# Two feed-forward column groups' first products among the last token transposes of a two-layer encoder, and half-sums formed per token tile

## The chip, the cores and the metric

One NeuronCore of a Trainium2 chip runs the whole two-layer network in one launch. The metric is the device time of one execution in microseconds (us), taken as the median over runs of the same program. Engines are written as in the profile: PE is TensorE, PEld its weight loads, DVE VectorE, ACT ScalarE, POOL GpSimd, SP the engine that issues the DMAs.

## The reference, cut to what matters

Each of two layers does, for 1024 tokens of width 1024 in float32:

```python
h = rms_norm(x, g_mix_pre)
u = h @ w_in                                   # attention, convolution, retention inputs
mix = jnp.concatenate([y_att, y_conv, y_ret], axis=-1) @ w_out
x = x + rms_norm(mix, g_mix_post)
h = rms_norm(x, g_mlp_pre)
f = jnp.square(jax.nn.relu(h @ w_up)) @ w_down # w_up: 1024 x 4096, w_down: 4096 x 1024
return x + rms_norm(f, g_mlp_post)
```

The change touches the stretch from `mix @ w_out` to the beginning of `h @ w_up`, in both layers.

## The kernel before

Tokens are worked on in eight tiles of 128 (t = 0 to 7); tiles 0 to 3 are the first token half, 4 to 7 the second. A float32 product is made of three matmuls on rounded parts: every operand is split into a high part (ACT casts it) and a low part (DVE subtracts the high part), and `mm3` (lines 147 to 151) issues high by high (L149), high weights by low moving (L150), low weights by high moving (L151).

**Output projection, right half.** The loop over the eight tiles under `Quarters(hblocks)` issues, for each tile, 24 matmuls of 128x512. Then the tile goes through a chain: ACT copies the result and sums its squares, DVE and POOL scale by the gain (`residual`, L235), POOL and DVE make the root-mean-square factor, DVE adds the residual (L240, with the old x loaded on SP's queue), ACT sums squares again, POOL makes the second factor, DVE scales to h (L208), PE transposes h in eight 128x128 blocks (L216), and ACT and DVE store the result (`Quarters.put`). The transposes carry a priority that moves them behind by `LAG`; a list scheduler, which simulates the program, places all instructions on each engine.

**Feed-forward up, `feed_up`.** The 1024x4096 weights are taken in eight column groups q of 512, and each group's product with h transposed is a fast 2x2 block product with seven half-size products instead of eight. The operands are quartered by row half and token half (`quarters.raw[j, n]`: row half j, token half n). Products 1 and 2 use the plain quarters of the first token half, so they need tiles 0 to 3 only. Products 3 to 7 use sums: on the moving side t1 to t4 and the plain quarter b22 (`moving_sums`, each 128x2048 sum and each split made as one DVE or ACT instruction, once per layer), on the weights' side s1, s2 and two more (`stationary_sums` and `last_sum`, four POOL instructions of 128x1024 per group, L290 and L287). One product is 24 matmuls of 128x512 into a pair of PSUM banks; a group is seven of them. The splits of weights and sums are all made by `parts_of` (ACT L294, DVE L295). `open_psum(4)` gives up all eight banks at once and takes them anew as four pairs a, b, c, d.

**Feed-forward down, `feed_down`.** It multiplies the seven results of each pair of groups, kept in DRAM, with the quarters of `w_down`; its accumulators are taken from the blocks of the feed-forward pool and first written by an ACT copy (L519).

Blocks are 128x2048 tiles of SBUF: 13 kept ones (`kb`), and 12 (`fb`) that live only in the feed-forward part. The mixer's result `mix` and the keys `kT` have their own pools per layer.

## Time and profile before

| | us |
|---|---|
| median of 3 runs | 2391.28 (2389.43 to 2391.61) |
| the profiled execution, its own time | 2391.76 |
| its span, first to last instruction | 2390.0 |
| PE busy | 2295.0 (96%) |
| DVE busy | 1630.6 (68%) |
| ACT busy | 1036.9 (43%) |
| POOL busy | 611.0 (26%) |
| mean granted clock of PE | 0.981 |

The page cuts the span into 40 slices of 59.75 us; a digit is the busy share in tenths. An idle time in the timeline stands in square brackets, with the instruction that ended it behind an arrow. A matmul's duration in the timeline is modelled and overlaps the next one's; the pace is read from the starts. The granted clock of 1.00 is 2.4 GHz, 0.50 is 1.2 GHz.

### The profile page before, as it was taken

What the parts mean: (1) busy time and instruction counts of PE and PEld (TensorE: products, weight loads), DVE (VectorE), ACT (ScalarE), POOL (GpSimd) and SP (SyncE); (2) the same over time, 40 slices, a digit from 0 to 9 for tenths busy, and PEclk for the clock granted to TensorE, in tenths of its full rate; (3) what the DMA queues carried; (4) which work ended last, traced back from release to release, by engine and by line L of the source; (5) the groups of instructions that cost most, each with busy time, mean ns of one, the idle gap of its engine ahead of it and who ended that gap; (6) DMA issues with size and microseconds to landing.
All of it is one profiled execution on the core that took longest, in us unless ns stands there. A gap on an engine that the chain in (4) does not pass through costs nothing.

```text
span 2390.0 us, 29843 instructions
## 1 busy us (share of the span) xinstructions
PE 2295.0 (96%) x11132; PEld 1885.7 (79%) x11132; DVE 1630.6 (68%) x2726; ACT 1036.9 (43%) x1745; POOL 611.0 (26%) x511
## 2 busy tenths in 40 slices
PE   8999999996999999999899999999969999999997
PEld 7887778775888887888788887787758888878886
DVE  6976776668554577577789676755785444766787
ACT  4234443564444454343332344535744444543332
POOL 1002222224565541000220122222245564400002
PEclk9999999997999999999999999999979999999998
DMA  5120110142344454434431210101424443554435
GB/s 180 49 67 6 32 36 1 54 150 88 136 173 146 154 209 178 176 123 159 154 116 49 67 32 5 36 1 54 168 75 171 145 159 138 211 185 159 146 137 167
DMA packets 108337, 268.29 MB, mean 112 GB/s; under 512 B 9608, under 2 KB 17824, under 8 KB 108192
## 3 DMA queue, kind: packets, MB, share of 16 engines
q1 hardware_dynamic: 108192, 266.39, 32.5%
q8 instruction: 87, 1.43, 0.3%
q14 instruction: 58, 0.48, 0.1%
HBM read 190.84 MB, written 75.52 MB: 111 GB/s over the span
## 4 chain that ended last, share of the span: by engine, by line
PE 41%; DVE 3%; issue 3%; POOL 2%; ACT 1%; DMA 1%; DVEq 0%; SPq 0%; ACTq 0%; POOLq 0%
PE pb L149 12%; PE pb L151 12%; PE pb L150 12%; PE pb L817 2%; DVE fb L240 1%; PE pb L804 1%; POOL kb L287 1%; PE pb L777 1%; PE pb L774 0%; PE pb L919 0%; PE pb L909 0%; POOL fb L287 0%; DVE fb L208 0%; POOL fb L290 0%; DVE kb L287 0%
## 5 line engine op out<-in xcount | busy, mean ns | idle before, releaser
L151 PE MATMUL pb<-kb,kb 128*128 128x512 f32 (+1 forms) x1600 | 623.7, 391 | 11.6 <-DVE kb L295 11.3
L149 PE MATMUL pb<-kb,kb 128*128 128x512 f32 (+1 forms) x1472 | 599.4, 409 | 5.5 <-ACT fb L519 2.4
L150 PE MATMUL pb<-kb,kb 128*128 128x512 f32 (+1 forms) x1536 | 598.8, 390 | 0.4 <-DVE kb L131 0.4
L290 DVE TENSOR_TENSOR fb<-pb,fb 128x1024 f32<-128x1024 f32 x174 | 212.7, 1223 | 276.4 <-PE pb L151 241.7
L151 PEld LDWEIGHTS pb<-kb,kb 128*128 128x128 f32 x1600 | 304.0, 190 | 74.2 <-DVE kb L295 13.6
L150 PEld LDWEIGHTS pb<-kb,kb 128*128 128x128 f32 x1536 | 293.6, 191 | 44.9 <-DVE kb L131 1.2
L149 PEld LDWEIGHTS pb<-kb,kb 128*128 128x128 f32 x1472 | 281.3, 191 | 58.1 <-issue 4.1
L149 PE MATMUL pb<-fb,kb 128*128 128x512 f32 x736 | 287.6, 391 | 13.9 <-ACT kb L294 13.9
L151 PE MATMUL pb<-fb,kb 128*128 128x512 f32 x704 | 273.7, 389 | 0.0
L150 PE MATMUL pb<-fb,kb 128*128 128x512 f32 x672 | 262.3, 390 | 1.3 <-DVE fb L295 1.3
L294 ACT CAST kb<-kb 128x1024 fp32r<-128x1024 f32 (+1 forms) x100 | 141.0, 1414 | 254.8 <-PE pb L150 150.1
L294 ACT CAST kb<-fb 128x1024 fp32r<-128x1024 f32 (+1 forms) x80 | 106.6, 1332 | 217.1 <-PE pb L150 134.8
L295 DVE TENSOR_TENSOR kb<-fb,kb 128x1024 fp32r<-128x1024 f32 (+1 forms) x72 | 139.2, 1933 | 77.0 <-ACT kb L294 76.9
L295 DVE TENSOR_TENSOR kb<-kb,kb 128x1024 fp32r<-128x1024 f32 (+1 forms) x78 | 152.0, 1951 | 37.5 <-ACT kb L294 37.4
L149 PEld LDWEIGHTS pb<-fb,kb 128*128 128x128 f32 x736 | 138.6, 188 | 43.1 <-ACT kb L294 14.7
L838 DVE SCALAR_TENSOR_TENSOR mix<-ypad,cw,mix 128x512 f32<-128x512 f32 x240 | 167.1, 751 | 1.0
L235 POOL TENSOR_TENSOR fb<-fb,fb 128x512 f32<-128x512 f32 x14 | 20.4, 1464 | 527.5 <-DMA fb<-in_norm_mlp_post_dram 254.1
L151 PEld LDWEIGHTS pb<-fb,kb 128*128 128x128 f32 x704 | 132.1, 188 | 27.5
L150 PEld LDWEIGHTS pb<-fb,kb 128*128 128x128 f32 x672 | 126.3, 188 | 28.5 <-DVE fb L295 2.3
L294 ACT CAST fb<-kb 128x2048 fp32r<-128x2048 f32 x42 | 80.3, 1913 | 112.5 <-DMA kb<-fd 59.2
L149 PE MATMUL pb<-kb,fb 128*128 128x512 f32 x320 | 124.5, 389 | 0.0
L131 DVE TENSOR_TENSOR kb<-kb,kb 128x512 fp32r<-128x512 f32 (+2 forms) x160 | 103.2, 658 | 28.2 <-ACT kb L130 26.1
(190 smaller groups left out, 4057.6 us busy)
## 6 DMA issues: line engine op xcount, KB each, us to landing
fd<-fb SPq DMA_DIRECT2D x80, 512.0 KB, 2.6
kb<-fd SPq DMA_DIRECT2D x36, 1024.0 KB, 4.9
fb<-in_w_up_dram SPq DMA_DIRECT2D x22, 1024.0 KB, 5.6
kb<-in_w_down_dram SPq DMA_DIRECT2D x44, 512.0 KB, 5.1
...
fb<-fd SPq DMA_DIRECT2D x20, 1024.0 KB, 5.0
fd<-kb SPq DMA_DIRECT2D x32, 512.0 KB, 3.5
kb<-in_w_up_dram SPq DMA_DIRECT2D x10, 1024.0 KB, 5.6
```

Source lines behind the costliest of these rows:

```text
L131: nc.vector.tensor_tensor(out=lo[:, :ncols], in0=raw[:, :ncols], in1=hi[:, :ncols].bitcast(F32), op=ALU.subtract)
L149: nc.tensor.matmul(ps, lhsT=a_hi, rhs=b_hi, start=first, stop=False, skip_group_check=more)
L150: nc.tensor.matmul(ps, lhsT=a_hi, rhs=b_lo, start=False, stop=False, skip_group_check=more)
L151: nc.tensor.matmul(ps, lhsT=a_lo, rhs=b_hi, start=False, stop=last, skip_group_check=more)
L240: nc.vector.scalar_tensor_tensor(out=xt[:, cs], in0=zs[c], scalar=r, in1=xt[:, cs], op0=ALU.mult, op1=ALU.add)
L287: eng.tensor_tensor(out=out, in0=a, in1=b, op=ALU.subtract)
L290: eng.tensor_tensor(out=out, in0=a, in1=b, op=ALU.add)
L294: nc.scalar.copy(hi, raw)
L295: nc.vector.tensor_tensor(out=lo, in0=raw, in1=hi.bitcast(F32), op=ALU.subtract)
L777: nc.tensor.matmul(ps[hh], lhsT=self.qs[hs, hh, :], rhs=klo[hs, ks], start=False, stop=True)
L817: nc.tensor.matmul(ops, lhsT=sb[:, j * P:(j + 1) * P], rhs=V[:, self.j0 + j, h * 64:(h + 1) * 64], start=j == 0, stop=j == nj - 1)
L838: nc.vector.scalar_tensor_tensor(out=acc, in0=src, scalar=cw[:, b, k:k + 1], in1=acc, op0=ALU.mult, op1=ALU.add)
```

## The change

Four things are changed.

1. `feed_up` becomes a class, `FeedUp`. Its method `early` makes products 1 and 2 of the groups 0 and 1 (four products) and stands among the transposes of tiles 6 and 7; `rest` makes the other products. PE's order in the projection loop is written by hand (`manual_schedule`): the transposes of tile t-2 follow the projection of tile t. Products 1 and 2 add up in PSUM for the groups 0 and 1, where a DVE addition stood for group 0.
2. `Quarters.put` forms t1 and t2 tile by tile for the second token half (L222 of the new file, eight DVE instructions of 128x512 per layer), in place of two of 128x2048. In `rest` the five moving splits are placed one by one, and the products come in the order 6, 5, 7, 3, 4 in place of 6, 7, 5, 4, 3.
3. The weights of group 0 are loaded during the projection loop (`weights_a` at tile 4, `weights_b` at tile 6), and a slice of group 1 by two more DMAs of 512 KB per layer, which read parts of what group 1's own load reads again.
4. Memory: PSUM is opened in four pools of one pair each, on two stacks. `mix`, the raw weights, the early results, and later four accumulators of `feed_down`, share two blocks of 128x4096 (`ma`, `mb`), `kT` and a weight block share `kk`; the `fb` blocks go from 12 to 7, and the accumulator "u" takes the head of the list of free blocks.

```diff
     class Quarters:
         def put(self, half, j, cs, ps):
-            nc.scalar.copy(quad(self.raw[j, half])[:, :, cs], ps)
+            raw = quad(self.raw[j, half])[:, :, cs]
+            nc.scalar.copy(raw, ps)
...
+            else:
+                t1 = quad(self.raw[0, 0])[:, :, cs]
+                out, sub = (t1, t1) if j == 0 else (quad(self.t2)[:, :, cs], t1)
+                nc.vector.tensor_tensor(out=out, in0=raw, in1=sub, op=ALU.subtract)
...
+    class FeedUp:
...
+        def weights_a(self):
+            self.mixa = doubles[0].two()
+            self.quarters.t2 = self.mixa[0]
+            self.r = [self.fetch(self.mixa[1], 0, 0)]
+            self.w1 = self.split(self.r[0][:, :, 0:256], self.wb[0])
+
+        def weights_b(self):
+            self.kraw = kblock.tile()
+            self.r.append(self.fetch(self.kraw, 1, 0))
+
+        def early(self, pairs):
+            wb, self.z, self.y = self.wb, *pairs
+            self.u = [halves(x) for x in doubles[1].two()]
+            first, second = self.quarters.parts[0], self.quarters.parts[1]
+            tmp = quad(wb[1].tile())
+            for j in range(2):
+                nc.sync.dma_start(out=tmp[:, :, 256 * j:256 * j + 256],
+                                  in_=w_up[self.l, j * 512:(j + 1) * 512, 512:768].rearrange("(a p) c -> p a c", p=P))
+            self.product(self.z, self.w1, first)
+            nc.scalar.copy(self.u[0][0], self.z)
+            v1 = self.split(tmp[:, :, 0:256], wb[2])
+            yield
+            self.product(self.y, v1, first)
+            nc.scalar.copy(self.u[1][0], self.y)
+            w2 = self.split(self.r[1][:, :, 0:256], wb[4])
+            v2 = self.split(tmp[:, :, 256:512], wb[3])
+            yield
+            for i, (ps, w) in enumerate(((self.z, w2), (self.y, v2))):
+                self.product(ps, w, second, True)
+                self.square(self.u[i][1], ps)
...
-                for t in range(NT):
-                    z = [z0[t], z1[:, t % 3, :]]
-                    for step in out_steps(wt, 1, t, z[1], 4, right_part):
-                        step()
-                    xt = load_x(t, x_cur, epool)
-                    residual(t, xt, z, sss[t], gpost, x_mid)
-                    h = epool.tile([P, D], F32, name="h")
-                    prenorm(t, xt, h, gpre, quarters, LAG)
+                with tc.manual_schedule(engines={mybir.EngineType.PE}):
+                    for t in range(NT):
+                        z = [z0[t], z1[:, t % 3, :]]
+                        for step in out_steps(wt, 1, t, z[1], 4, right_part):
+                            step()
+                        if t >= 2:
+                            turn_tile(t - 2, normed.pop(t - 2), quarters)
+                        if t == 4:
+                            up.weights_a()
+                        if t == 6:
+                            up.weights_b()
+                        finish(t, z)
+                    early = up.early(as_pairs(0))
+                    for t in (6, 7):
+                        next(early)
+                        turn_tile(t, normed.pop(t), quarters)
+                    for _ in early:
+                        pass
...
             if name not in acc:
-                own, acc[name] = take(F32, False)
                 if name == "u":
-                    ublock = own
+                    ublock, acc["u"] = take()
+                elif name == "c11":
+                    acc["c11"], acc["c12"] = doubles[0].two()
+                elif name == "c22":
+                    acc["c21"], acc["c22"] = doubles[1].two()
```

PE, first layer, from the end of the projection on, before. `h` rows are transposes; a product's rows read PSUM pair, moving operand, weights; `fb_5412` and `fb_5413` are t3's high and low part, `fb_5403` t2's high part, `kb_5336` product 1's weights.

```order
L216 MATMUL pb_7_76<-ident,h 128x128
L149 MATMUL pb_2_5334<-kb_4775,kb_5337 128x512
...
L151 MATMUL pb_2_5334<-kb_4775,kb_5337 128x512
L149 MATMUL pb_0_5332<-kb_4773,kb_5336 128x512
L150 MATMUL pb_0_5332<-kb_4774,kb_5336 128x512
L149 MATMUL pb_3_5335<-fb_5412,kb_5337 128x512
L150 MATMUL pb_3_5335<-fb_5413,kb_5337 128x512
L149 MATMUL pb_1_5333<-fb_5403,kb_5338 128x512
L151 MATMUL pb_0_5332<-kb_4773,kb_5336 128x512
```

All transposes of tiles 6 and 7 stand ahead of the first product, and two rows of product 7 stand inside product 1.

The same place after. `pb_2_1_85` is the last tile's projection, `pb_0_0_5326` the pair of group 0 and `pb_1_0_5330` that of group 1; `kb_4779` and `kb_4781` are the plain quarters; `fb_5497` and `fb_5498` are t1's parts, `fb_5490` and `fb_5491` t2's.

```order
L181 MATMUL pb_2_1_85<-kb_90,ks_5259 128x512
L260 MATMUL pb_3_1_80<-ident,h 128x128 x4
L179 MATMUL pb_0_0_5326<-kb_4779,kb_5098 128x512
...
L179 MATMUL pb_1_0_5330<-kb_4779,kb_5360 128x512
...
L179 MATMUL pb_0_0_5326<-kb_4781,kb_5400 128x512
...
L179 MATMUL pb_1_0_5330<-kb_4781,kb_5403 128x512
...
L179 MATMUL pb_3_0_5481<-fb_5497,kb_5528 128x512
L180 MATMUL pb_3_0_5481<-fb_5498,kb_5528 128x512
L179 MATMUL pb_2_0_5485<-fb_5490,kb_5494 128x512
L180 MATMUL pb_2_0_5485<-fb_5491,kb_5494 128x512
L181 MATMUL pb_3_0_5481<-fb_5497,kb_5528 128x512
```

Four whole products come before the first one that needs a sum, with the transposes of tiles 6 and 7 behind the first and the second of them; after the fourth, two rows of product 5 and two of product 6 stand ahead of product 5's rest.

DVE, first layer, around the last tile, before: h of tile 7, then the three 128x2048 sums and the splits.

```order
L208 SCALAR_TENSOR_TENSOR h<-xt,rstd_5308,ks_4767 128x1024
L287 TENSOR_TENSOR kb_4769<-kb_4770,kb_4769 128x2048
L287 TENSOR_TENSOR fb_5399<-kb_4772,kb_4769 128x2048
L287 TENSOR_TENSOR kb_4770<-kb_4772,kb_4770 128x2048
L295 TENSOR_TENSOR fb_5413<-kb_4769,fb_5412 128x2048
L287 TENSOR_TENSOR kb_4771<-kb_4771,fb_5399 128x2048
L295 TENSOR_TENSOR kb_5336<-fb_5340,kb_5336 128x1024
```

After (`kb_5360` and `kb_5403` are group 1's weights, read from the slice `kb_5332`; L284 is tile 7's residual; `kb_4775` is t1 and `ma` t2):

```order
L339 TENSOR_TENSOR kb_5360<-kb_5332,kb_5360 128x1024
L284 SCALAR_TENSOR_TENSOR xt<-V,rstd2h,xt 128x512
...
L339 TENSOR_TENSOR kb_5403<-kb_5332,kb_5403 128x1024
...
L247 SCALAR_TENSOR_TENSOR h<-xt,rstd_5318,ks_4773 128x1024
L222 TENSOR_TENSOR kb_4775<-kb_4776,kb_4775 128x4x128
L222 TENSOR_TENSOR ma<-kb_4778,kb_4775 128x4x128
L331 TENSOR_TENSOR kb_4776<-kb_4778,kb_4776 128x2048
L331 TENSOR_TENSOR kb_4777<-kb_4777,ma 128x2048
L339 TENSOR_TENSOR fb_5498<-kb_4775,fb_5497 128x2048
L339 TENSOR_TENSOR fb_5491<-ma,fb_5490 128x2048
L339 TENSOR_TENSOR kb_5528<-fb_5486,kb_5528 128x1024
```

Group 1's low parts now stand ahead of tile 7's residual and h; behind h there are two pieces of 128x512, the sums t3 and t4, and then the low parts of t1, t2 and product 5's weights.

SP's queue in the first layer, before and after (tile loads `xt`, tile stores `x_mid`, weights `in_w_up`):

```order
L193 DMA xt<-in_x_dram 128x1024 x2
L242 DMA x_mid_319<-xt 128x512 x2
L193 DMA xt<-in_x_dram 128x1024
L242 DMA x_mid_319<-xt 128x512 x4
L337 DMA fb_5340<-in_w_up_dram 128x4x512
```

```order
L286 DMA x_mid_328<-xt 128x512 x3
L359 DMA kk<-in_w_up_dram 128x4x512
L286 DMA x_mid_328<-xt 128x512
L232 DMA xt<-in_x_dram 128x1024 x2
L381 DMA kb_5332<-in_w_up_dram 128x4x256 x2
L286 DMA x_mid_328<-xt 128x512 x4
```

A 1 MB weight load now stands ahead of the loads of tiles 6 and 7, and the slice of group 1 directly behind them.

## Rows read from the trace of the kernel before

**Rows 1.** The page, 40 slices of the span: PE's busy tenths.

```profile
PE   8999999996999999999899999999969999999997
```

**Rows 2.** The waits of PE over the whole span: total us, times, longest us.

```profile
PE pb L216 <- DVE h L208: 20.7, 3, 9.3
PE pb L149 <- ACT kb L294: 15.2, 4, 7.1
PE pb L151 <- DVE kb L295: 11.3, 4, 4.3
```

**Rows 3.** Timeline of PE, first layer: start, us, instruction, count, idle before.

```profile
545.53 1.06 PE L216 MATMUL pb<-ident,h 128*128 128x128 f32 x8 [2.29 <-DVE ms2h L222]
552.30 1.97 PE L216 MATMUL pb<-ident,h 128*128 128x128 f32 x8 [5.70 <-DVE h L208]
...
568.77 0.80 PE L149 MATMUL pb<-fb,kb 128*128 128x512 f32 x1 [6.84 <-ACT kb L294]
570.20 0.80 PE L150 MATMUL pb<-fb,kb 128*128 128x512 f32 x1 [0.63 <-DVE fb L295]
...
575.71 0.80 PE L151 MATMUL pb<-kb,kb 128*128 128x512 f32 x1 [4.29 <-DVE kb L295]
```

**Rows 4.** Stretches: us, busy (count) of PE, PEld, DVE, ACT, POOL, clock, DMA.

```profile
500.00:540.00 40.00, 39.91 (x194) 32.10 (x193) 34.32 (x60) 30.02 (x63) 9.21 (x19) 1.00 0.49 168
...
548.00:554.00 6.00, 1.70 (x9) 1.71 (x9) 2.06 (x3) 1.15 (x2) 0.74 (x2) 0.50 0.82 264
554.00:557.00 3.00, 3.00 (x9) 2.37 (x8) 2.29 (x1) 1.07 (x2) 2.06 (x1) 0.50 0.94 352
...
562.00:576.00 14.00, 2.31 (x4) 1.09 (x5) 14.00 (x5) 7.03 (x5) 10.36 (x3) 0.60 0.00 0
576.00:582.00 6.00, 6.00 (x15) 4.67 (x15) 6.00 (x4) 1.91 (x1) 0.00 (x0) 0.52 0.01 1
582.00:588.00 6.00, 6.00 (x28) 4.90 (x28) 5.74 (x4) 1.96 (x2) 0.00 (x0) 1.00 0.12 22
```

**Rows 5.** Timeline of PE at the same place of the second layer.

```profile
1757.11 0.80 PE L149 MATMUL pb<-fb,kb 128*128 128x512 f32 x1 [7.07 <-ACT kb L294]
```

**Rows 6.** Timeline of ACT and DVE: the chain of the last tile, some of its links.

```profile
542.90 0.56 ACT L619 COPY U<-pb 128x512 f32<-128x512 f32 x1
543.50 0.69 DVE L235 TENSOR_TENSOR U<-U,V 128x512 f32<-128x512 f32 x1 [1.74 <-ACT U L619]
...
550.96 1.28 DVE L208 SCALAR_TENSOR_TENSOR h<-xt,rstd,ks 128x1024 f32<-128x1024 f32 x1 [2.17 <-POOL rstd L144]
```

**Rows 7.** Timeline of PE at full clock: two matmuls of a product in succession.

```profile
640.80 0.39 PE L149 MATMUL pb<-fb,kb 128*128 128x512 f32 x1
641.03 0.39 PE L150 MATMUL pb<-kb,kb 128*128 128x512 f32 x1
```

**Rows 8.** Timeline of DVE and POOL, and POOL's group by line (count, busy, mean ns).

```profile
561.33 4.46 DVE L287 TENSOR_TENSOR kb<-kb,kb 128x2048 f32<-128x2048 f32 x1
...
563.59 4.41 POOL L287 TENSOR_TENSOR fb<-fb 128x1024 f32<-128x1024 f32 x1
...
574.44 1.21 DVE L295 TENSOR_TENSOR kb<-fb,kb 128x1024 fp32r<-128x1024 f32 x1
575.57 2.28 DVE L295 TENSOR_TENSOR fb<-fb,fb 128x2048 fp32r<-128x2048 f32 x1
...
L287 POOL TENSOR_TENSOR kb<-kb 128x1024 f32<-128x1024 f32 x4 | 9.6, 2399 | 0.0
```

**Rows 9.** The page's DMA issues: count, KB each, median us from issue to landing.

```profile
kb<-in_w_down_dram SPq DMA_DIRECT2D x44, 512.0 KB, 5.1
...
fb<-in_w_up_dram SPq DMA_DIRECT2D x22, 1024.0 KB, 5.6
```

**Rows 10.** Timeline of PE at the start of feed-forward down, both layers.

```profile
899.89 0.50 PE L149 MATMUL pb<-kb,kb 128*128 128x512 f32 x1 [1.20 <-ACT fb L519]
...
2087.97 0.50 PE L149 MATMUL pb<-kb,kb 128*128 128x512 f32 x1 [1.21 <-ACT fb L519]
```

More of the change, by code (lines that the diff above doesn't have):

```diff
@@ L66, with open_psum, as_banks, as_pairs @@
     places = {"d": [0, 1], "s": [2, 3], "r": [4, 5], "o": [6], "t": [7]}
-    pool_now = []
-    banks = []
-    def open_psum(n):
-        if pool_now:
-            pool_now.pop().release()
-        pool = tc.alloc_tile_pool(name="psum", bufs=1, space=PSUM, reuse_waits="tile")
-        pool_now.append(pool)
-        return [pool.tile([P, 4096 // n], F32, name=f"pb{n}_{i}") for i in range(n)]
-    banks.extend(open_psum(8))
-    ctx.callback(lambda: pool_now.pop().release())
+    pools, banks = {}, {}
+    def open_psum(order, n):
+        for i in reversed(order):
+            if i in pools:
+                pools.pop(i).release()
+        got = []
+        for i in order:
+            pools[i] = tc.alloc_tile_pool(name=f"psum{i}", bufs=1, space=PSUM, reuse_waits="tile",
+                                          side="left" if i < 2 else "right")
+            got.append([pools[i].tile([P, 1024 // n], F32, name=f"pb{n}_{i}_{j}") for j in range(n)])
+        return got
+    STACKS = ([0, 1], [3, 2])
+    def as_banks():
+        for order in STACKS:
+            for i, pair in zip(order, open_psum(order, 2)):
+                banks[2 * i], banks[2 * i + 1] = pair
+    def as_pairs(which):
+        return [pair[0] for pair in open_psum(STACKS[which], 1)]
+    as_banks()
+    ctx.callback(lambda: [pools[i].release() for i in (1, 0, 2, 3)])
     def bank(tag):
@@ L431, in feed_down, with take @@
         free = list(free)
-        def take(dt=F32, passing=True):
-            i = 0 if passing else next(i for i, b in enumerate(free) if not b.stays)
-            b = free.pop(i)
+        def take(dt=F32):
+            b = free.pop(0)
             return b, b.tile(dt)
@@ L534, in feed_down @@
             gpre = load_gain(None, g_mix_pre, l + 1, "gpre", halves(gains)[1])
-            mykept = [b for b in free if b.stays]
+            mykept = [b for b in free if b.stays and b is not kblock]
             assert len(mykept) == len(kept), (len(mykept), len(free))
@@ L700, in rows @@
         def rows(k, half):
-            return mix[:, 4 * half:4 * half + 4, k, :]
+            return mix[half][:, :, k, :]
         def v4(ap):
@@ L948, in ret_out @@
             nc.tensor.transpose(out=ops, in_=y, identity=ident)
-            nc.scalar.copy(mix[:, t, 2 + p, :], ops)
+            nc.scalar.copy(mix[t // 4][:, t % 4, 2 + p, :], ops)
         def nxt(g):
```

268 lines of the change are left out of this document (150 added, 118 removed).

## The prediction, made before the changed kernel ran

> **What bounds the kernel now.** I read the page first. PE is busy nearly everywhere; two inner slices of 40 fall to 6 tenths [rows 1], at 538 to 598 us and 1673 to 1733 us, where the output projection ends and feed-forward up begins, once per layer. The list of PE's waits says the same: its three largest sums are for h of a tile (20.7 us, of which 9.3 are the program's start), for a cast and for a low part [rows 2]. The timeline puts them into one stretch of 33 us: 2.29 and 5.70 us for the chains of tiles 6 and 7, then 6.84, 0.63 and 4.29 us for casts and low parts of sums and weights, 19.75 us in all [rows 3]. The second layer has the same five waits with 7.07 in place of 6.84 [rows 5], 19.98 us. The stretches show two things more. DVE is busy all 14 us of 562 to 576 while PE is busy 2.31: behind tile 7 the bound is DVE's queue. And the granted clock is 0.50 at 554 to 557 and near it at 576 to 582, after the idle times, against 1.00 at 582 to 588 [rows 4].
>
> The price of the half clock, from rows: the transposes at 552.30 take 1.97 us where those at 545.53 take 1.06, 0.9 lost [rows 3]; 576 to 582 holds 15 matmuls and the next 6 us 28, so 13 x 0.23 = 3.0 us are lost, and 554 to 557 holds 9 where 14 fit, 1.1 lost at 0.23 us per matmul [rows 4, 7]. That is 5.0 us. **Lost per layer now: 19.8 + 5.0 = 24.8 us.** The rest of the two slices is work.
>
> **The change part by part.** Let zero be the end of the last projection matmul (542.6 in the trace). PE's work is unchanged: a product is 24 x 0.227 = 5.4 us, eight transposes some 0.8 to 1.06.
>
> *Four products among the transposes.* The new order has transposes of tile 5, a product, tile 6, a product, tile 7, two products. Products 1 and 2 need tiles 0 to 3 alone, so PE has 21.8 us of products where it waited. A tile's chain takes 9.7 us: from 542.6 through the copy at 542.90 to the end of h at 552.24 [rows 6]. Tile 6's projection ends some 6.4 us before zero, so its h is due at 3.3, and PE comes for it at 0.8 + 5.4 = 6.2: hidden, with 2.9 to spare. PE comes for tile 7 at 6.2 + 0.8 + 5.4 = 12.4, against 9.7. But on DVE six instructions now stand between this chain's links: two low parts of 1.21 [rows 8] and four pieces of 0.69 [rows 6], 5.2 us. Those that fall into the chain's ACT and POOL links are free. The wait is between 0 and 9.7 + 5.2 - 12.4 = 2.5 us; I take 1.5, since the two low parts stand directly ahead of tile 7's residual and h.
>
> *The loads.* The weight load of 1 MB and the x tiles now share SP's queue in another order. Tile 6's x is behind 1 MB, 5.6 us [rows 9]; its h has 2.9 us to spare, so this hides. The slice of group 1, 2 x 512 KB, is issued behind tile 7's x, which frees its buffer when tile 5's h is made, about 3 us before zero; at 5.1 us [rows 9] it lands near 2.3, and with a cast and a low part of about 1.2 each [rows 8] is split at 4.7. PE needs it at 7.0. Nothing shows a load of these short runs; between twice as fast and twice as slow (7.4) it costs nothing up to 2.7 us.
>
> *The sums.* This is what is late next. Behind h of tile 7, DVE has: two pieces, t3, t4, low part of t1, low part of t2, low part of the weights of product 5. POOL's four weight sums of 128x1024 come at the same time: they stand behind POOL's factor of tile 7 and so begin at 11. Side by side a DVE instruction of 2048 takes 4.46 us and a POOL one 4.41; alone 2.28 and 2.40 [rows 8]. So POOL is at work from 11 to 11 + 2.4 + 3 x 4.4 = 26.6. DVE: transposes at 13.9, ACT's copy 0.6, the pieces (1.3 each beside POOL) to 17.5, t3 to 21.9, t4 to 26.3, low t1 to 28.9 (mostly alone), low t2 to 31.2, the weights' to 32.4. PE: 13.9 + 0.8 + 2 x 5.4 = 25.5 and then needs these three in just this order, one matmul after each of them. It waits 28.9 - 25.5 = 3.4, then 2.1, then 1.0: **6.5 us**. From there on products 5, 6 and 7 give PE 15.6 us of work; the low parts of t3, b22 and t4 (2.28 each) and those of three more weights follow within 11 us: hidden. Bounds: 0 if DVE got through first (a rival below), 11 if all three are at the doubled length.
>
> *The transposes by hand.* In the loop, those of tile t-2 follow the projection of tile t: 12.8 us behind the end of tile t-2's projection against a chain of 9.7. DVE is busy 34.3 of 40 us there [rows 4]; the t1 and t2 pieces of tiles 4 to 7 replace as many subtractions for the first half, and two more low parts come in. 0 to 3 us per layer, I take 1.
>
> *The clock.* Idle times of 3.4, 2.1 and 1.0 us within 8 us may halve it again. Between nothing and the 3.0 of 576 to 582; I take 1.5.
>
> *Start of feed-forward down.* PE waits 1.20 us and 1.21 us for the first ACT copy into accumulator "u" [rows 10]. That copy's block is now one that was free long before. Gain 1.2 per layer; what the freed 1.2 us uncovers is the DMA-fed split behind it, so between 0 and 1.2; I take 1.2.
>
> *No price.* The four added DMAs (two per layer, 512 KB) besides what is said above: the stretch 562 to 576 has an idle DMA [rows 4]. PSUM in four pools: the pairs of the early products were last used by tiles 5 and 6, and PE reaches them after tile 7's projection. The DVE addition that is gone for group 0 (1.2 us) was off PE's path. `mix` and `kT` in shared blocks: their next writers come after the accumulators were read; 0 to 2 us at the layers' border, I take 0.
>
> **Sum.** Lost per layer after: 1.5 + 6.5 + 1 + 1.5 = 10.5 us. Gain per layer 24.8 - 10.5 = 14.3, twice 28.6, with 2 x 1.2 at feed-forward down 31.0. The profiled execution took 2391.76 us (span 2390.0), so 2360.8; the median of the runs is 0.5 lower: **2360 us**, 1.3% faster. With every bound at its good end the layer loses nothing: 2391.8 - 2 x 26 = 2340. At its bad end it loses 2.5 + 11 + 3 + 3 + 2.7 = 22.2: 2386.
>
> **The rivals.**
>
> *The sums cost more: DVE's queue is the new bound.* If POOL goes on beside DVE through all three low parts, they end at 30.7, 35.1 and 37.4 (4.4, 4.4, 2.3): the waits come to 11.6 us in place of 6.5, with the clock's 3.0, 17 us per layer. Gain 2 x 7.7 + 2.4 = 18: 2373. For it: in the trace DVE took 4.3 to 4.5 us for each of four such instructions while POOL had work. Against it: POOL has only four here, and they begin before DVE's do.
>
> *DVE gets through first.* If DVE's queue, which is never empty here, is not held up by POOL, its pieces, sums and low t1 need 1.4 + 3 x 2.28 = 8.2 us and end at 22.7, low t2 at 25.0, the weights' at 26.2: PE waits under 1 us, and the clock stays. Lost per layer 3.5 us, gain 2 x 21.3 + 2.4 = 45: 2347. The trace has both slowed by as much [rows 8], so it speaks against it. The Trainium skill, "SBUF — State Buffer", section "Who interferes with whom", says that a DVE instruction with two SBUF inputs and a POOL instruction that reads SBUF contend for one pair of ports, and that whoever issues first holds it for the whole instruction; by that rule a queue that always issued first would give this case, and 2347. The trace agrees with the lock (4.46 is near 2.28 + 2.40) but shows the two taking turns.
>
> *It does not do what it says.* If the slice of group 1 lands some 15 us later than I have it, its low part, which stands ahead of tile 7's residual on DVE, delays both the second product and tile 7, and the waits are back: 2388 to 2391. Needed is a landing time of 20 us where 5.1 to 5.6 are seen [rows 9].
>
> *Slower.* PE's order is now fixed in the projection loop: a late h stops the next tile's projection too, which the scheduler's order had let go ahead. The six transposes of the loop each have 3.1 us to spare. If the chains there grew from 9.7 to 16.5, because DVE, busy 86% [rows 4], falls behind with each tile, each would stop PE 3.7 us: 6 x 3.7 = 22 us per layer less the 1 counted, against 14.3 gained. With the lower clock (3.0) that is 2 x (21 + 3 - 14.3) - 2.4 = 17 us slower: 2409. It decides from 2.6 us per stop. Against it: DVE has 0.9 us of each 6.4 free, and the change adds 3.6 us over the last four tiles.
>
> **How the numbers follow.** Forecast (2352 to 2369) 0.62; sums cost more (2369 to 2386) 0.16; DVE first (2340 to 2352) 0.12; no effect 0.04; slower 0.06. A range of 2345 to 2377 holds the forecast, over half of each neighbour (some 0.09 and 0.11): 0.82. A difference under 0.2% (4.8 us) cannot be told from none. Faster by more (under 2386.5) is 0.62 + 0.16 + 0.12 = 0.90, the same 0.04, slower 0.06.
>
> **What would show it.** After the last projection PE should have no wait over 3 us up to the fourth product, then three waits in a row, each for a DVE low part, the first the longest, and no DVE instruction ahead of tile 7's h for long. The cast wait of 6.84 should be gone, and so the 1.20 for the first copy in feed-forward down. Wrong would be: waits at the transposes inside the projection loop; a second product that waits for a DMA; a clock of 0.50 for over 7 us; new waits in the mixer of the second layer.

## The result and the profile after

The changed kernel takes **2349.25 us**, the median of four runs (2347.58 to 2351.52), against 2390.36 for the kernel before in runs beside it (2389.23 to 2391.61): a ratio of **0.9829, with a 95% interval of 0.9812 to 0.9846**. It is faster, the time lies inside the range on record and 10.75 us under the forecast. The profiled execution took 2347.58 us (span 2345.8).

The page: PE's busy tenths and its clock in 40 slices, to hold beside [rows 1].

```profile
PE   8999999999999999999999999999999999999997
PEclk9999999999999999999999999999999999999998
```

The two slices of 6 tenths are gone. The waits of PE over the whole span (us, times, longest us), to hold beside [rows 2]:

```profile
PE pb L260 <- DVE h L247: 12.6, 3, 8.3
PE pb L260 <- ACT fb L225: 5.5, 1, 5.5
...
PE pb L180 <- DVE fb L339: 4.1, 4, 1.5
...
PE pb L181 <- DVE ks L706: 1.5, 4, 0.6
```

The wait for casts, the second largest of before, is not in the list, and of the 12.6 us for h, 8.3 are the program's start; the lines left out are for other stages. New is one of 5.5 us, the longest that is left behind the start; it stands at the border of the layers. The timeline of PE in the transition of the first layer (start, us, instruction, idle before it and for whom), to hold beside [rows 3]:

```profile
549.50 1.03 PE L260 MATMUL pb<-ident,h 128*128 128x128 f32 x8
...
558.19 1.73 PE L260 MATMUL pb<-ident,h 128*128 128x128 f32 x8 [2.17 <-DVE h L247]
...
572.59 0.50 PE L180 MATMUL pb<-fb,kb 128*128 128x512 f32 x1 [0.56 <-DVE fb L339]
574.79 0.50 PE L180 MATMUL pb<-fb,kb 128*128 128x512 f32 x1 [1.47 <-DVE fb L339]
575.92 0.79 PE L181 MATMUL pb<-fb,kb 128*128 128x512 f32 x1 [0.63 <-DVE kb L339]
```

Tile 6 is turned without a wait (549.50), tile 7 after 2.17 us, and behind the fourth product stand the three waits that the prediction named, 2.66 us in all (2.69 in the second layer). Stretches of the same place (busy us of PE, PEld, DVE, ACT, POOL; granted clock; DMA), to hold beside [rows 4]:

```profile
555.00:560.00 5.00, 2.83 (x14) 2.33 (x13) 3.42 (x2) 1.65 (x3) 4.92 (x2) 0.85 0.00 0
560.00:566.00 6.00, 6.00 (x24) 4.81 (x24) 5.90 (x3) 4.70 (x4) 5.99 (x3) 0.84 0.00 0
...
572.00:578.00 6.00, 3.34 (x9) 2.17 (x9) 6.00 (x5) 5.44 (x6) 0.00 (x0) 0.80 0.22 87
```

DVE hardly pauses from 560 on: behind tile 7 its queue is the bound, as predicted. The clock is below 1.00 twice, after the wait for tile 7 and after the three waits. What DVE and POOL do there, to hold beside [rows 8]:

```profile
554.69 2.37 POOL L334 TENSOR_TENSOR fb<-ma,kk 128x1024 f32<-128x1024 f32 x1
557.13 3.23 POOL L331 TENSOR_TENSOR fb<-fb,ma 128x1024 f32<-128x1024 f32 x1
560.31 2.84 POOL L331 TENSOR_TENSOR ma<-ma 128x1024 f32<-128x1024 f32 x1
563.12 2.87 POOL L331 TENSOR_TENSOR kk<-kk,fb 128x1024 f32<-128x1024 f32 x1
...
554.75 3.38 DVE L247 SCALAR_TENSOR_TENSOR h<-xt,rstd,ks 128x1024 f32<-128x1024 f32 x1 [0.44 <-POOL rstd L174]
559.72 1.19 DVE L222 TENSOR_TENSOR kb<-kb,kb 128x512 f32<-128x512 f32 x1 [1.58 <-ACT kb L214]
561.01 2.69 DVE L222 TENSOR_TENSOR ma<-kb,kb 128x512 f32<-128x512 f32 x1
563.63 4.50 DVE L331 TENSOR_TENSOR kb<-kb,kb 128x2048 f32<-128x2048 f32 x1
568.05 2.28 DVE L331 TENSOR_TENSOR kb<-kb,ma 128x2048 f32<-128x2048 f32 x1
570.26 2.28 DVE L339 TENSOR_TENSOR fb<-kb,fb 128x2048 fp32r<-128x2048 f32 x1
```

These ten rows carry what follows. POOL's first sum begins at 554.69, 0.06 us ahead of h of tile 7. Its 2.37 us are its single length; h takes 3.38 us where the h of tile 6 (546.76) took 1.28, which is 2.3 of standing still and 1.1 of work. Then it goes the other way round: POOL's second sum begins at 557.13 while h runs to 558.13, and takes nearly 2.37 and that rest. The piece at 561.01 takes 2.69 because POOL's third sum runs to 563.15, and t3 takes 4.50, the rest of the fourth sum and its own 2.28. Once POOL is done, at 565.99, t4 takes 2.28. Against their lengths alone (1.28, 0.69, 0.69, 2.28) the four DVE instructions beside POOL's four sums take 2.10, 0.50, 2.00 and 2.22 us longer: 6.8 us in which DVE stands still.

Two places outside the transition moved as well. At the start of feed-forward down the waits of [rows 10] are gone, and with them the two behind them in the trace of before: 0.15 and 1.36 at 911.25 and 913.58, 1.10 and 1.36 in the second layer. At the border of the layers the waits have grown, from 2.52 + 0.46 + 3.45 = 6.43 us to 5.51 + 0.25 + 3.10 = 8.86. PE there, before:

```profile
1187.72 1.07 PE L216 MATMUL pb<-ident,fb 128*128 128x128 f32 x8 [2.52 <-ACT fb L186]
1189.25 0.62 PE L149 MATMUL pb<-kb,kb 128*128 128x384 f32 x1 [0.46 <-ACT kb L168]
...
1193.64 1.12 PE L216 MATMUL pb<-ident,fb 128*128 128x128 f32 x4 [3.45 <-DVE kb L169]
```

And after:

```profile
1169.96 1.94 PE L260 MATMUL pb<-ident,fb 128*128 128x128 f32 x8 [5.51 <-ACT fb L225]
1172.15 0.69 PE L179 MATMUL pb<-kb,kb 128*128 128x384 f32 x1 [0.25 <-ACT kb L198]
...
1176.26 1.12 PE L260 MATMUL pb<-ident,fb 128*128 128x128 f32 x4 [3.10 <-DVE kb L199]
```

**The balance of the two traces.** They differ by 44.2 us. The clock's price in a stretch is PE's busy time in it times what the clock lacks to 1.00: in the first layer of before 5.20 x 0.47 (547 to 557.5) and 8.31 x 0.47 (564 to 582), 6.4 us; after, 3.81 x 0.43 (558 to 562) and 3.37 x 0.43 (575 to 579), 3.1 us, in the second layer 4.3. With the waits (19.75 and 19.98 before; 0.58 + 2.17 + 2.66 and 0.57 + 2.17 + 2.69 after) the transitions lost 26.1 and 26.3 us before (the second layer at the clock of the first) and lose 8.5 and 9.8 after: 34.1 us gained. Feed-forward down gives 2.7 and 3.7 us, the border takes 2.4. That is 38.1. Most of the rest lies in the second layer's mixer, whose waits behind the border are alike to some tenths of a us: the clock of before was 0.96 in 40 us and 0.98 in 200 us of it, that of after 1.00, 5.4 us. The median times differ by 41.1, for the profiled execution of before was 1.4 us over its median and that of after 1.7 under.

### The profile page after: what moved, and what is told of

Same layout as the page of the kernel before. It is cut to its first block, busy times and chain, and to the rows that moved or that the text cites. A ratio compares the mean times of both kernels' runs of the same rounds, so it can differ in the third digit from the quotient of the medians.

```text
span 2345.8 us, 29804 instructions
## 1 busy us (share of the span) xinstructions
PE 2284.0 (97%) x11132; PEld 1878.7 (80%) x11132; DVE 1621.5 (69%) x2736; ACT 1032.1 (44%) x1745; POOL 606.7 (26%) x511
## 4 chain that ended last, share of the span: by engine, by line
PE 45%; DVE 2%; ACT 1%; issue 1%; DMA 1%; POOL 0%; DVEq 0%; ACTq 0%; POOLq 0%; SPq 0%
PE pb L179 13%; PE pb L181 13%; PE pb L180 13%; PE pb L939 2%; PE pb L926 1%; DVE fb L284 1%; PE pb L899 1%; PE pb L896 0%; PE pb L260 0%; PE pb L1041 0%; PE pb L1031 0%; PE pb L1039 0%; PE pb L1047 0%; PE pb L1070 0%; DMA kb<-in_w_out_dram 0%
## 5 line engine op out<-in xcount | busy, mean ns | idle before, releaser
L179 PE MATMUL pb<-kb,kb 128*128 128x512 f32 (+1 forms) x1760 | 706.5, 403 | 1.9 <-ACT V L1085 1.1
L181 PE MATMUL pb<-kb,kb 128*128 128x512 f32 (+1 forms) x1792 | 693.1, 388 | 0.0
L180 PE MATMUL pb<-kb,kb 128*128 128x512 f32 (+1 forms) x1632 | 632.3, 388 | 0.9 <-DVE kb L161 0.9
L181 PEld LDWEIGHTS pb<-kb,kb 128*128 128x128 f32 x1792 | 337.3, 188 | 66.8 <-DVE kb L161 0.4
L179 PEld LDWEIGHTS pb<-kb,kb 128*128 128x128 f32 x1760 | 332.5, 189 | 63.8 <-issue 4.5
L180 PEld LDWEIGHTS pb<-kb,kb 128*128 128x128 f32 x1632 | 309.0, 189 | 48.9 <-DVE kb L161 1.9
L180 PE MATMUL pb<-fb,kb 128*128 128x512 f32 x576 | 226.0, 392 | 4.1 <-DVE fb L339 4.1
L181 PE MATMUL pb<-fb,kb 128*128 128x512 f32 x544 | 213.5, 393 | 1.2 <-DVE kb L339 1.2
L179 PE MATMUL pb<-fb,kb 128*128 128x512 f32 x480 | 188.3, 392 | 0.0
L338 ACT CAST kb<-fb 128x2048 fp32r<-128x2048 f32 (+1 forms) x70 | 105.7, 1519 | 120.9 <-PE pb L181 65.8
L338 ACT CAST kb<-kb 128x2048 fp32r<-128x2048 f32 (+1 forms) x62 | 96.2, 1551 | 139.2 <-PE pb L181 72.6
L180 PEld LDWEIGHTS pb<-fb,kb 128*128 128x128 f32 x576 | 109.1, 189 | 28.5 <-DVE fb L339 5.8
L334 DVE TENSOR_TENSOR mb<-pb,mb 128x1024 f32<-128x1024 f32 x56 | 68.4, 1221 | 85.6 <-PE pb L181 85.6
L339 DVE TENSOR_TENSOR kb<-kb,kb 128x1024 fp32r<-128x1024 f32 (+1 forms) x50 | 102.8, 2057 | 34.8 <-ACT kb L338 30.2
L181 PEld LDWEIGHTS pb<-fb,kb 128*128 128x128 f32 x544 | 103.2, 190 | 23.4 <-DVE kb L339 1.9
L160 ACT CAST kb<-kb 128x512 fp32r<-128x512 f32 (+2 forms) x160 | 90.3, 576 | 68.2 <-PE pb L180 36.1
L179 PEld LDWEIGHTS pb<-fb,kb 128*128 128x128 f32 x480 | 91.3, 190 | 19.0
L939 PEld LDWEIGHTS pb<-V,sb 128*128 128x128 f32 x720 | 93.8, 191 | 12.4 <-DVE att_o L941 2.5
```

The lines of the kernel that those rows point to most:

```text
L160: nc.scalar.copy(hi[:, :ncols], raw[:, :ncols])
L179: nc.tensor.matmul(ps, lhsT=a_hi, rhs=b_hi, start=first, stop=False, skip_group_check=more)
L180: nc.tensor.matmul(ps, lhsT=a_hi, rhs=b_lo, start=False, stop=False, skip_group_check=more)
L181: nc.tensor.matmul(ps, lhsT=a_lo, rhs=b_hi, start=False, stop=last, skip_group_check=more)
L334: eng.tensor_tensor(out=out, in0=a, in1=b, op=ALU.add)
L338: nc.scalar.copy(hi, raw)
```

## The experiments

Each changes the changed kernel, but for one that starts from the kernel before. The theory behind them: **DVE and POOL take turns at two-input instructions, each holding the other up for its whole length, and DVE's queue behind tile 7 sets when PE goes on.** The rivals: the wait for tile 7 comes of the six instructions between the chain's links, as the prediction had it; t3 and t4 are needed as early as the low parts; the queue is simply too long. The kernel before was run beside each set; its medians were 2389.16 to 2389.44. The changed kernel was run only in the set of the result, where the kernel before had 2390.36. A difference to the changed kernel is given as one of medians; by the ratios to the kernel before it is 0.6 to 2 us other.

**1. POOL's sums behind h of tile 7.**

```
+                    if t == NT - 1:
+                        up.gate = nc.gpsimd.tensor_copy(small.tile([P, 1], F32, name="gate"), normed[t][:, 0:1]).ins
...
-            stationary_sums(r)
+            with tc.issue_after(self.gate):
+                stationary_sums(r)
```

> The four POOL sums of group 0's weights begin only when h of tile 7 is made (a 128x1 copy of h on POOL stands ahead of them); all else as in the changed kernel. Theory A (the two engines take turns, an instruction of one holds the other for its whole length): h of tile 7 takes 1.28 us in place of 3.38 and PE's wait of 2.17 for its transposes goes. But the same four sums, 4 x 2.4 us, now lie between DVE's later instructions: t3, t4 and perhaps the low part of t1 take 4.5, and PE's three waits behind the fourth product grow from 2.66 to some 6 us. Net per layer between 0 and 2 us lost: 2349 to 2354. Theory B (the wait of 2.17 comes from the two low parts and four pieces that stand between the chain's links, and POOL's sum only fills the gap): h is still late, the wait stays at 1.5 to 2.2, and the three waits grow as above: 2354 to 2360.

Measured: 2352.0 us (2350.45 to 2353.49), ratio to before 0.9846 (0.9831 to 0.9860), not told apart from the changed kernel. POOL and DVE, and behind them PE's waits:

```profile
558.02 2.38 POOL L334 TENSOR_TENSOR fb<-ma,kk 128x1024 f32<-128x1024 f32 x1
...
556.53 1.28 DVE L247 SCALAR_TENSOR_TENSOR h<-xt,rstd,ks 128x1024 f32<-128x1024 f32 x1 [0.44 <-POOL rstd L174]
...
563.69 4.49 DVE L331 TENSOR_TENSOR kb<-kb,kb 128x2048 f32<-128x2048 f32 x1
568.11 4.49 DVE L331 TENSOR_TENSOR kb<-kb,ma 128x2048 f32<-128x2048 f32 x1
...
574.85 0.80 PE L180 MATMUL pb<-fb,kb 128*128 128x512 f32 x1 [4.75 <-DVE fb L339]
577.05 0.79 PE L180 MATMUL pb<-fb,kb 128*128 128x512 f32 x1 [0.98 <-DVE fb L339]
578.19 0.79 PE L181 MATMUL pb<-fb,kb 128*128 128x512 f32 x1 [0.34 <-DVE kb L339]
```

h takes 1.28 us, PE turns tile 7 without a wait, and the three waits are 6.07 us in place of 2.66. So the wait for tile 7 was POOL's first sum; the six instructions of the chain stand where they stood and cost no wait by themselves. They do not leave anything to spare either: h is done at 557.81, and PE comes for it at 557.87. And taking it away won nothing: the sums now fall beside t3 and t4, both 4.49, and what tile 7 gained is waited for some 17 us later.

**2. Low parts ahead of t3 and t4 on DVE.**

```
+                    needed = lows[-3:]
...
-                    moving(7)
-                    sub(V, t4, t4, t2)
+                    with ExitStack() as behind:
+                        for i in needed:
+                            behind.enter_context(tc.issue_after(i))
+                        moving(7)
+                        sub(V, t4, t4, t2)
```

> DVE makes the low parts of t1, t2 and the weights of products 5 and 6 ahead of the sums t3 and t4; POOL as in the changed kernel. Theory A (turns; the three waits of 2.66 us are the queue of DVE, of which t3 and t4 are 6.8 us that no one needs yet): POOL's last sum now holds the low part of t1, 4.5 us, to about 568; the others end near 570.5 and 573, PE is through with the fourth product at 572, so the waits shrink to under 0.5 us, and the wait of 2.17 for tile 7 stays. 2.2 to 2.7 us per layer, up to 4.4 with the clock: 2340 to 2345. Theory B (the sums of t3 and t4 are needed just as soon): the waits come back one or two products later, at t3 or t4, with as much: 2348 to 2351.

Measured: 2343.38 us (2341.19 to 2345.27), 0.9810 (0.9793 to 0.9826); its runs lie under all of the changed kernel's. DVE's queue, and a stretch of the core:

```profile
564.66 4.50 DVE L339 TENSOR_TENSOR fb<-kb,fb 128x2048 fp32r<-128x2048 f32 x1
...
573.55 2.28 DVE L331 TENSOR_TENSOR kb<-kb,kb 128x2048 f32<-128x2048 f32 x1
...
572.00:578.00 6.00, 6.00 (x28) 4.96 (x27) 6.00 (x5) 5.10 (x5) 0.00 (x0) 1.00 0.45 180
```

POOL's last sum falls on the low part of t1 and makes it 4.50, as expected, and still PE has no wait behind the fourth product: 28 matmuls in 6 us at the full clock. t3 and t4 were not needed yet. The wait for tile 7 stays, 2.16 us. Later one wait comes back, in the first layer 1.50 us at 596.17 and in the second 0.39 at 1759.86; in the first it is for the cast of a sum of the next group that POOL, which took 5.35 us for the sum before, finished late.

**3. Without POOL's four sums.**

```
-            stationary_sums(r)
...
-                last_sum(r)
+                if q > 0:
+                    last_sum(r)
```

> POOL's four sums of group 0's weights are left out (products 5, 6, 7 and 3 of that group take unsummed weights, so the output is another); all else as in the changed kernel. It measures what these four sums cost together. Theory A (turns): DVE's instructions of this stretch are back at their single lengths, h 1.28, pieces 0.69, t3 2.28; DVE is 6.8 us earlier at the low parts, both the wait of 2.17 and the three of 2.66 go; 4.8 us per layer and up to 3.4 of clock: 2333 to 2340. Theory B (DVE's queue alone is the bound, POOL's sums cost it little): the waits shrink by less than half, 2344 to 2349.

Measured: 2335.08 us (2334.4 to 2336.84), 0.9776 (0.9761 to 0.9791): 14.2 us under the changed kernel, 7.1 per layer, though DVE makes t3 and t4 ahead of the low parts as in the changed kernel. That is the price of four POOL sums that no row of PE ever names: the waits of 2.17 and 2.66 us and the clock's 3.1 to 4.3, less 0.68 that is left at tile 7 and 0.35 at 585.

**4. The sums on DVE.** Two right behind h of tile 7, two behind `needed`, in the order of experiment 2.

```
-            stationary_sums(r)
+            a11, a21, a12, a22 = quarters_of(r)
+            with tc.issue_after(self.gate):
+                add(V, s1, a21, a22)
+                sub(V, s2, s1, a11)
...
+                        sub(V, a21, a11, a21)
                         moving(7)
                         sub(V, t4, t4, t2)
+                        sub(V, a12, a12, s2)
```

> The four sums of group 0's weights are made by DVE (1.2 us each, two right behind h of tile 7, two behind the low parts of products 5 and 6) in place of POOL, and DVE makes those low parts ahead of t3 and t4, as in the second experiment. Theory A (the two engines take turns, so a POOL sum costs DVE 2.4 us where DVE's own would cost it 1.2): h of tile 7 1.28 us, no wait for its transposes over 0.7 us, none behind the fourth product over 0.5 us; as without the sums, 2333 to 2338. Theory B (DVE's queue is too long for four more instructions): 4.8 us more on DVE come back as waits at products 7, 3 or 4, 2340 to 2345.

Measured: **2334.44 us** (2333.24 to 2335.75), 0.9775 (0.9761 to 0.9790), 14.8 us under the changed kernel and the best of all. DVE, and the stretches:

```profile
555.00 1.28 DVE L247 SCALAR_TENSOR_TENSOR h<-xt,rstd,ks 128x1024 f32<-128x1024 f32 x1 [0.44 <-POOL rstd L174]
556.20 1.22 DVE L334 TENSOR_TENSOR fb<-ma,kk 128x1024 f32<-128x1024 f32 x1
...
555.00:560.00 5.00, 4.94 (x26) 3.92 (x25) 4.56 (x5) 3.69 (x5) 0.00 (x0) 1.00 0.01 2
...
572.00:578.00 6.00, 6.00 (x28) 4.95 (x28) 6.00 (x5) 1.20 (x2) 0.00 (x0) 1.00 0.23 91
```

DVE has four instructions more, of 1.22 us each, and has the low parts of products 5 and 6 ready 23.5 us behind the transposes of tile 5 (543.41), where in experiment 2 it took 29.4. The four cost it 4.9 us of work where POOL's cost it 6.8 of standing still, and two of them lie behind these low parts. PE has no wait from 543 to 590, and the clock stays at 1.00. With experiment 2 beside it, order alone is worth 5.9 us and the sums on DVE, with two of the four behind the low parts, 8.9 more; the engine and the place of those two were not tried apart. The wait for tile 7 is gone though the six instructions still stand in its chain, which confirms experiment 1.

**5. POOL's sums split.** Two behind h of tile 7, the other two behind low parts that DVE makes, each held by a 128x1 copy on POOL. In this kernel t4 is made after u3 has been written over t2, so its values are others; the instructions and their lengths are those of the kernel.

```
+            with tc.issue_after(self.gate):
+                add(G, s1, a21, a22)
+                sub(G, s2, s1, a11)
...
+                    gated(w[1], a21, a11, a21)
...
+                    gated(rows[7][1], a12, a12, s2)
```

> Both at once and one thing more: POOL makes the two sums that products 5 and 6 need behind h of tile 7, the other two only behind DVE's low parts of these products, and DVE makes everything in the order in which PE needs it. Theory A: h of tile 7 1.28 us, no wait at its transposes, no wait over 0.5 us behind the fourth product, 4.8 us per layer gained, and 1.5 to 3.4 more if the clock then stays at 1.00: 2333 to 2340. Theory B (DVE's and POOL's work behind tile 7 is simply longer than the products that cover it): one of products 7, 3 or 4 waits 2 us or more, and half of the gain at most is left: 2344 to 2350.

Measured: 2351.73 us (2349.98 to 2353.15), 0.9844 (0.9830 to 0.9859): nothing gained. ACT and PE:

```profile
573.36 1.05 ACT L338 CAST kb<-ma 128x1024 fp32r<-128x1024 f32 x1 [2.73 <-POOL ma L331]
575.28 1.89 ACT L338 CAST fb<-kb 128x2048 fp32r<-128x2048 f32 x1
...
590.66 0.76 PE L179 MATMUL pb<-kb,kb 128*128 128x512 f32 x1 [4.66 <-DVE ma L334]
```

Up to 580 PE has no wait and the clock is 1.00, as theory A has it. Then the late sums come due. ACT's cast of the weights from POOL (573.36) stands ahead of the cast of t3 (575.28), DVE is idle 6.12 us until that is made, and PE waits 0.63 and 4.66 us, and 1.25 at 600.47. Theory B is nearer in the time, though hardly by the length of the work: experiment 4 makes the same sums, on DVE, and has no wait over 0.5 us in this stretch. The rows point to the order on ACT and POOL that the edit made; that order was not tried by itself.

**6. The early products behind all transposes.**

```
                     for t in (6, 7):
-                        next(early)
                         turn_tile(t, normed.pop(t), quarters)
                     for _ in early:
```

> The changed kernel with the four early products behind the transposes of tiles 6 and 7, so only their place among the transposes is undone. Theory A (the placement hides the chains of tiles 6 and 7; the products behind them then hide all sums): PE waits some 2.3 and 5.7 us for the two tiles as before, at the lower clock afterwards, and not behind the fourth product: 8 + 1 to 2 lost against 2.2 + 2.7 + 1.7 to 3.4 now, so 1 to 4 us per layer dearer, 2351 to 2357. Theory B (the placement carries most of the gain): 2365 to 2380.

Measured: 2362.09 us (2358.12 to 2362.87), 0.9885 (0.9869 to 0.9902): 12.8 us over the changed kernel, 6.4 per layer, between the two theories' times.

```profile
550.29 1.94 PE L260 MATMUL pb<-ident,h 128*128 128x128 f32 x8 [3.98 <-DVE ms2h L268]
...
560.25 1.97 PE L260 MATMUL pb<-ident,h 128*128 128x128 f32 x8 [8.02 <-DVE h L247]
```

The waits are 12.0 us and not the 8.0 of before, and there is none behind the fourth product. The chain itself has become longer: h of tile 7 takes 3.35 us here too, since POOL's sums begin ahead of it, which explains 2.1 of the 2.3 us that tile 7 waits longer. So the place among the transposes carries 6.4 of some 17 us per layer. The rest falls to the other parts of the change, among them the four products that PE has before the sums are due at all; but for experiment 7 it was not taken apart.

**7. t1 and t2 as whole sums again.**

```
-            else:
-                t1 = quad(self.raw[0, 0])[:, :, cs]
-                out, sub = (t1, t1) if j == 0 else (quad(self.t2)[:, :, cs], t1)
-                nc.vector.tensor_tensor(out=out, in0=raw, in1=sub, op=ALU.subtract)
...
+            sub(V, t1, t3, t1)
+            sub(V, t2, b22, t1)
```

> The changed kernel with t1 and t2 made as two sums of 2048 columns behind the last transposes, as before the change, in place of tile by tile; the early products stay. Theory A (DVE's queue behind tile 7 sets when PE goes on): two sums of 2.28 us stand where two pieces of 0.69 stood, 3.2 us more, and 5.4 if one of POOL's sums falls beside them; the three waits of 2.66 us in all become 6 to 8, 3 to 5.5 us per layer lost: 2355 to 2360. Theory B (these sums are as well hidden behind the four products): 2348 to 2351.

Measured: 2356.26 us (2353.73 to 2364.25), 0.9867 (0.9845 to 0.9890): 7 us dearer, 3.5 per layer; in the first layer PE waits 4.13 us at 574.35 for a low part and 2.86 at 594.99 for an addition behind it, 7.0 us in place of 2.66, in the second 2.73 and 2.85. Theory A. The pieces earn what they save on DVE behind tile 7; in the projection loop they cost nothing, for the loop's wait is the same with them and without (0.58 and 0.56), and they do not hold up tile 7: its h begins 11.6 us behind the first transposes after the projection with them and 11.7 without.

**8. In the kernel before, only the block of u.**

```
-                own, acc[name] = take(F32, False)
+                own, acc[name] = take(F32, name == "u")
```

> The kernel before with one argument changed: accumulator u of feed-forward down takes the block that has been free longest, as in the changed kernel, and nothing else. Theory A (the waits at the start of feed-forward down, 1.20 and 1.36 us, both hang on the first ACT copy into that block): both go in both layers, 4 to 6.5 us in all, 2383 to 2386.5. Theory B (only the 1.20 hangs on it; the 1.36 for a low part goes by other means): 2.4 us, 2387 to 2388.5.

Measured: 2385.62 us, the median of ten (2383.37 to 2389.24), 0.9988 (0.9979 to 0.9998), 0.5 to 5 us gained. The waits of [rows 10] and those behind them are gone, but another has come in each layer:

```profile
912.70 0.50 PE L149 MATMUL pb<-fb,fb 128*128 128x512 f32 x1 [2.09 <-ACT fb L519]
...
2095.34 0.50 PE L149 MATMUL pb<-fb,fb 128*128 128x512 f32 x1 [2.60 <-ACT fb L519]
```

It is for the same line's copy into a later accumulator. By the waits the edit is worth 0.6 and 1.1 us; the time's interval holds both theories. In the changed kernel the later accumulators too have blocks of their own (`ma`, `mb`), and neither wait is there.

**9. At the border, the last additions first.**

```
+            with tc.issue_after(last_add) if t >= 2 else ExitStack():
+                residual(t, xt, z, ss, gpost, x_dst)
+                prenorm(t, xt, h, gpre, ht, LAG)
```

> At the border of the layers DVE makes the two last additions into the accumulators (they read out the pair of PSUM into whose place the transposes of the second layer go) ahead of the residual of tiles 2 to 7; all else as in the changed kernel. Theory A (PE's wait of 5.51 us at 1169.96 is for that addition, which stands behind four residual pieces on DVE, and not for ACT's square sum): the second addition begins some 3.4 us earlier and the wait falls to about 2 us; the wait of 3.10 behind it may grow by 1: 2 to 3.5 us gained, 2345.5 to 2347.5. Theory B (the wait is for the normed tile): it stays at 5 to 5.5, or the next wait grows by as much: 2349 to 2350.

Measured: 2350.43 us (2347.86 to 2352.33), 0.9841 (0.9827 to 0.9856), the same as without. PE at the border, and then in the transition of the first layer:

```profile
1167.65 1.07 PE L260 MATMUL pb<-ident,fb 128*128 128x128 f32 x8 [1.41 <-DVE mb L624]
...
573.54 0.50 PE L180 MATMUL pb<-fb,kb 128*128 128x512 f32 x1 [2.20 <-DVE fb L339]
575.75 0.80 PE L180 MATMUL pb<-fb,kb 128*128 128x512 f32 x1 [1.47 <-DVE fb L339]
576.88 0.79 PE L181 MATMUL pb<-fb,kb 128*128 128x512 f32 x1 [0.34 <-DVE kb L339]
...
555.00:572.00 17.00, 14.18 (x66) 11.26 (x64) 15.09 (x7) 9.69 (x9) 11.86 (x5) 1.00 0.19 62
```

The cause of the 5.51 us is shown: the releaser is now the addition itself, and its wait is 1.41 us. But later waits take its place: behind 0.46 and 2.25 us there are 0.55 at 1182.01, 0.46 at 1185.36 and 1.53 at 1187.51, where the changed kernel has none, so that the border's waits are 6.66 us in place of 8.86. That the time did not fall by these 2 us either is not explained by them; this trace has the clock under 1.00 in the second layer's mixer (0.83 in 1520 to 1540), which the trace of the changed kernel has not, and that is more. What the edit is worth stays open.

The last rows are worth more than the border. The transition's code is untouched, and its three waits are 4.01 us where the changed kernel's trace has 2.66. The clock tells why: 1.00 in 555 to 572, where the changed kernel had 0.85 and 0.84. PE was through with its products sooner and waited longer. Counted from the start of tile 7's h (555.68 here, 554.75 there), it goes on at 21.20 and at 21.17 us. DVE's queue sets that moment, and a us that the clock takes ahead of it comes out of the wait.

**10. Experiments 4 and 9 together.**

> Group 0's sums on DVE in the order in which PE needs them, and at the layers' border the last two additions ahead of the residual of tiles 2 to 7. Theory A (two separate causes, so the gains add): the transition without waits as before, 14 to 15 us under the changed kernel, and at the border 4 us of waits fewer (8.5 to some 4.5): 2329 to 2332. Theory B (the border's gain is given back at a later stage, as the time of the border experiment alone would have it): 2333 to 2336.

Measured: 2336.86 us (2335.93 to 2338.31), 0.9780 (0.9765 to 0.9794). Theory B, and a little over experiment 4. The border's waits are 1.41 + 0.46 + 2.64 + 0.46 + 4.02 = 9.0 us, where experiment 4 has 8.5: here a later pair of transposes waits 4.02 us at 1182.98, the one that waits 1.53 in experiment 9. So the border has not been mended; experiment 4 alone is the version to keep.

## Why the prediction was right, and where it was off

**The bound** was read rightly: the chains of tiles 6 and 7 ahead, DVE's queue behind, the clock besides. Experiments 6 and 7 undo two parts of the change and give back 6.4 and 3.5 us per layer.

**What the kernel before lost** was put at 24.8 us per layer, and its clock at 5.0 of them, counted from matmuls in three stretches. By PE's busy time under the lower clock it is 6.4, 1.4 per layer more to be won.

**Tile 6** was hidden, as said. **Tile 7** waits 2.17 us against 1.5 (0 to 2.5): the number was near by luck and its reason wrong. The prediction itself let POOL begin its sums "behind POOL's factor of tile 7", which is the moment at which h begins, and priced the two beside each other only from the pieces on. Experiments 1 and 4 show that without this collision there is no wait. The chain had grown all the same: from zero (here the first transposes behind the projection, 543.16) h would have been made at 12.9 us, not 9.7, had it taken its single 1.28, and PE came at 12.9. What the change put into the chain thus used up the slack, and every us of the collision was one for PE.

**The loads** cost nothing: no PE row in the transition waits for a DMA.

**The sums** are the mis-sized term: 6.5 us in the forecast, 2.66 and 2.69 measured. Its working can be laid beside the rows, with the same zero. Forecast for the ends of the pieces, t3, t4, the low parts of t1, t2 and of the weights: 17.5, 21.9, 26.3, 28.9, 31.2, 32.4. Measured: 20.5, 25.0, 27.2, 29.4, 31.6, 32.7. The end is right to 0.3 us, because two errors cancel. POOL's sums were all put at 4.4 us, which is their length beside an instruction of 2048 columns; beside short pieces they took 2.84 to 3.23, POOL was done at 22.8 and not 26.6, and t4 ran alone. Against that, h and the pieces were held up by 2.1 and some 2.5 us. So DVE's end, on which the waits hang, was right, and the step that failed is PE's arrival: 25.5 in the forecast, 28.9 measured. Of the 3.4 us between them, 0.7 are the longer wait for tile 7 and 1.6 the lower clock behind that wait (3.81 us of busy PE at 0.57), which the forecast had only behind the three waits; the rest is work, such as eight transposes at 1.03 us that were put at 0.8. The three waits are what is left between PE's arrival and DVE's end, and so they were shorter by about as much. Experiment 9's trace shows the same from the other side: at a clock of 1.00 PE came earlier and waited 4.01.

**The transposes by hand** cost 0.58 us against 1, with a smaller wait for the same line 0.75; **the clock** 3.1 and 4.3 against 1.5, in the first layer 1.6 ahead of the three waits and some 1.5 behind them, which is where the forecast had its 1.5. In all the layer loses 8.5 and 9.8 us after the change against 10.5 forecast.

**Feed-forward down** was put at 1.2 per layer, with 1.2 as its upper bound, and gave 2.7 and 3.7. The bound was wrong: it took the wait behind the first copy for one that freed time would uncover, and did not look at the blocks of the other accumulators, which the change moved too. Experiment 8 has u alone, and a wait of 2.1 to 2.6 us for the next one.

**The border** was put at 0 (0 to 2) and cost 2.4. The mechanism was not seen: on DVE the last additions into the accumulators stand behind four residual pieces, and PE's transposes wait for them.

**The rivals.** The time lies in the interval of "DVE gets through first", but that mechanism is not there: h at 3.38 and t3 at 4.50 were held up. Experiment 3 is that rival made real, and gives 2335; some 7 of the 12 us under its 2347 are the clock of before and feed-forward down, priced too low. On its rule the Trainium skill ("SBUF — State Buffer", section "Who interferes with whom") says that a DVE instruction with two SBUF inputs contends with POOL's reads, and speaks of the pair of ports as a lock held for a whole instruction. The rows agree: 3.38 is 2.31 of waiting for a sum of 2.37 and the work of h, which has two such inputs. "Sums cost more" was a matter of all four low parts beside POOL, and POOL was done before the first. The stops in the projection loop ("slower") did not come; by that rival's own sum they would have decided from 2.3 us each and not from 2.6.

In sum, against the profiled execution the forecast was 13.2 us too high: 5.5 in the transitions (34.1 in place of 28.6: 2.8 for the clock of before, 2.7 for shorter waits less a dearer clock), 4.0 at feed-forward down, 5.4 in the mixer's clock, with which the change has nothing to do, less 2.4 at the border, and 0.7 that is not assigned. Between the medians it is 10.75.

## What to carry to other kernels

Work given to POOL to relieve DVE can cost DVE more than doing it: here four sums cost 6.8 us of standing still that DVE makes in 4.9, and 2.1 of them fell on the one instruction that PE came for. The row that shows it is not a wait but a duration, 3.38 or 4.50 where the same instruction takes 1.28 or 2.28 elsewhere. Before pricing an engine's queue as the bound, look in which order it makes what is needed, and price a wait as the gap between two arrivals: what the waiting engine loses ahead of it makes it shorter. Whoever frees one buffer at the start of a stage should ask for the next buffer in the same line.

## What the runs showed besides

A sum on POOL is longer by what is left of DVE's instruction, and the other way round, to within 0.2 us: 2.37 alone, 2.84 to 3.24 beside instructions of 512 or 1024 columns, 4.45 beside one of 2048. One row of experiment 2 goes beyond that: a sum at 587.23 takes 5.35 us, through the rest of one DVE instruction with two SBUF inputs (to 589.17) and the whole of the next (to 590.31). The rule of thumb "both double" of [rows 8] holds only where both queues are full of instructions of like length.

The clock falls in places that no edit touches. The same mixer of the second layer, first in the trace of before and then of after, in stretches of like work:

```profile
1445.00:1645.00 200.00, 195.00 (x1171) 156.15 (x1171) 134.83 (x527) 92.52 (x273) 47.81 (x78) 0.98 0.08 25
```

```profile
1424.00:1624.00 200.00, 195.28 (x1192) 156.10 (x1192) 136.54 (x533) 94.98 (x281) 48.37 (x78) 1.00 0.08 25
```

It is some 3 to 4 us in this stretch, as much as a small edit is worth here. A gain of that size has to be read from the waits of its own place and not from two traces' ends; why the clock falls there in one execution and not in another was not tried.
